# Rotating the latent queries of a two-layer encoder: the exchange of halves as copies out of PSUM instead of a product, with the rotated dimensions projected first

## The chip, the cores and the metric

The kernel runs on one core of one Trainium2 chip. The core's engines work side by side, each through its own queue of instructions in a fixed order: TensorE (PE, matrix products into the 8 banks of PSUM), VectorE (DVE), ScalarE (ACT), GpSimd (POOL) and SyncE (SP), which here issues nearly all of the transfers. The metric is the device time of one execution in microseconds (us), as a median over runs.

## The reference

The model is a bidirectional encoder trunk of two layers on 256 tokens of width 2048, all in fp32. In each layer four heads of differential attention and eight heads of latent attention share an input projection and an output projection; a dense MLP with squared ReLU follows, and every sublayer is modulated by a conditioning vector `c`. The part that the change touches is the latent attention's query: 512 latent columns `cq` are normalised and projected to eight heads of 128 plain ("nope") and 64 rotated dimensions.

```python
q = (_rmsnorm(cq, q_norm_g[l]) @ w_uq[l]).reshape(B, S, MLA_HEADS, MLA_NOPE + MLA_ROPE)
q_nope = q[..., :MLA_NOPE]
q_rope = _rope(q[..., MLA_NOPE:], cos[:, :, None, :], sin[:, :, None, :])
...
def _rope(x, cos, sin):
    half = x.shape[-1] // 2
    x1, x2 = x[..., :half], x[..., half:]
    out = jnp.concatenate([x1 * cos - x2 * sin, x2 * cos + x1 * sin], axis=-1)
    return out.astype(x.dtype)
```

So each 64-vector is split into halves of 32, which change places for the sine's term. The scores are `(q_nope . k_nope + q_rope . k_rope) / sqrt(192)`, with one rotated key `k_rope` for all heads. `mod = silu(c) @ w_ada[l] + b_ada[l]` gives the modulation, 12288 values in each layer.

## The kernel before

**Weights.** fp32 precision is had from three products of a faster format: each 1 MB weight tile `raw` comes by one transfer (issued by SyncE) and is split in two halves of 128x1024. ScalarE writes the rounded `hi` (L148), VectorE the remainder `lo = raw - hi` (L151), and PE multiplies `hi` with the rounded activation, `hi` with its remainder and `lo` with the rounded activation (L187 to L189; L258 to L260 where the tokens are the stationary side). `weights()` does the load and the split. There are 5 `raw` buffers and 4 each of `hi` and `lo`.

**The modulation runs beside the rest.** `w_ada` is 192 tiles of 1 MB, called `ada`, which use the same 5 buffers as `raw`. VectorE multiplies each with `silu(c)` and sums it (L304), and after every second tile adds the bias to `mod` (L315, L317). Each call of `weights()` does two things at its end: `ada_sums(ins)` sums all `ada` tiles loaded so far and orders those sums behind the second `lo` of this weight; then `self.credit += self.rate` decides how many new `ada` loads are issued behind it. The rate is set by stage: 0.7 in most of layer 0, 2.7 while `up_q(0)` loads its weight there, 1.7 in the value stages. So where a weight stands in the program also decides where `ada` loads stand in SyncE's queue and where their sums stand in VectorE's.

**The place of the change.** In each layer, after the differential heads' scores, the program goes through these steps: `up_k()` projects the plain keys; `probs(3)` is the softmax of the last differential head; `up_q(0)` projects the plain query dimensions of the first four latent heads; `turn(0)` transposes the first head's probabilities (PE into bank `pt`, L1187, then a copy `aT`); `up_r()` projects all rotated query dimensions, 4 x 128 columns in two banks `pss`, copies each bank to `qr` on ScalarE with the scale of the scores (`copy`, L277), and calls `rope_q` on it; `turn(1)`; `mla[0]()`, the first latent head's scores; `up_v()`, the latent value weights `w_uv` (banks `pv`, copies `vm`); the next heads; `up_q(1)`; and then the differential values, eight weights `w_dv` interleaved with the other latent heads, called the value stage below.

`rope_q` (L1131 to L1141) exchanges the halves by a product on PE with a constant 128x128 permutation, kept among the constants that one transfer brings (tile `tab`): the fp32 product takes `qr` 128x512 into a bank `pqr` (L1135). VectorE multiplies that bank with the sine into `qrt` (L1138), `qr` with the cosine (L1139), and adds the two (L1140).

`mla_steps` writes a latent head's scores into one bank `psm` in two halves of 128 queries: plain part (L1235, `kn`, `qn`), rotated part (L1236, `kr`, `qr`), and VectorE negates and reduces each half into `sm` (L1237). ScalarE's exponential follows (L1149). The second half's product and the first half's reduction use the same bank, and PE waits for that reduction before it goes on with the second half.

**The order.** Each engine's order is fixed when the program is built. In layer 0 a scheduler with its own estimates of durations interleaves the steps, within the dependencies; `follow(ins, after)` adds one by hand, without a semaphore, for order alone. In layer 0 the `hi` copies of `w_uv` follow `self.copied`, the last call of `copy`.

Of the kernel before, what the change touches and what calls it, by code (L numbers as in the profile page):

```python
# [13 lines left out]
AF = mybir.ActivationFunctionType  # L14
ALU = mybir.AluOpType
AX = mybir.AxisListType

P = 128
# [21 lines left out]
]  # L40

C_DELTA = 0
C_PERM = 32
C_CB = 160
C_W2 = 168
C_FREQ = 176
C_SGN = 177
NCONST = 178

V_BADA = 0  # L50
V_SUBLN = 192
# [19 lines left out]
def consts():  # L71
    c = np.zeros((P, NCONST), np.float32)
    p = np.arange(P)
    c[p, C_DELTA + p % 32] = 1.0
    c[p, C_PERM + (p ^ 32)] = 1.0
    for g in range(8):
        for r in range(4):
            b = 4 * g + r
            n = b % 16
            lo, hi = BUCKET_FROM[n], BUCKET_FROM[n + 1] - 1  # L80
            sign = -1.0 if b < 16 else 1.0
            rows = slice(32 * r, 32 * r + 32)
            if b == 16:
                c[rows, C_CB + g], c[rows, C_W2 + g] = 0.0, 0.0
            else:
                c[rows, C_CB + g] = -sign * (lo + hi) / 2.0
                c[rows, C_W2 + g] = 1.0 if n < 8 else ((hi - lo) / 2.0 + 0.25) ** 2
    c[:, C_FREQ] = np.asarray(INV_FREQ, np.float32)[p % 32]
    c[:, C_SGN] = np.where(p % 64 < 32, -1.0, 1.0)
    return c  # L90
# [13 lines left out]
class Trunk:  # L104
# [231 lines left out]
    def setup(self):  # L336
# [4 lines left out]
        nc.sync.dma_start(row, io["c"])  # L341
        tab = cp.tile([P, T + 8 + NCONST + NVEC], F32, name="tab")
        nc.scalar.dma_start(tab, io["tab"])
        self.pos = tab[:, : T + 8].bitcast(I32)
        self.K = tab[:, T + 8 : T + 8 + NCONST]
        self.vec = tab[:, T + 8 + NCONST :]
        self.x = cp.tile([P, NK, T], F32, name="x")
# [94 lines left out]
    def bias_part(self, a):  # L442
# [8 lines left out]
        for g in order[:4]:  # L451
            sqs.append(self.t("sq"))
            ins = nc.scalar.activation(sqs[-1], r, AF.Square, bias=K[:, C_CB + g : C_CB + g + 1])
        if a < 3:
            self.rel[a + 1] = self.distances(a + 1)
        self.bias_out(ins)
        for g in order:
            if g % 4 > 1:
                sq = sqs.pop(0)
            else:  # L460
                sq = self.t("sq")
                nc.scalar.activation(sq, r, AF.Square, bias=K[:, C_CB + g : C_CB + g + 1])
            oh = half("oh", F32R)
            flat, edge = sq.rearrange("p a b -> p (a b)"), K[:, C_W2 + g : C_W2 + g + 1]
            if g % 4 < 2:
# [27 lines left out]
    def rope_setup(self):  # L493
# [3 lines left out]
        nc.vector.tensor_copy(ang, pos[:, :T])  # L497
        nc.vector.tensor_scalar(ang, ang, K[:, C_FREQ : C_FREQ + 1], None, ALU.mult)
        magic = 1.5 * 2.0**23
# [15 lines left out]
        nc.scalar.activation(self.cos, c, AF.Sin)  # L515
        nc.vector.tensor_scalar(self.sin, self.sin, K[:, C_SGN : C_SGN + 1], None, ALU.mult)

# [187 lines left out]
    def layer(self, l, acc, st):  # L705
        nc, io = self.nc, self.io
        qs = 1.0 / math.sqrt(128.0)
        ms = 1.0 / math.sqrt(192.0)
# [16 lines left out]
        else:  # L725
            h = acc
            lat = []
            for b in range(0, NAHEAD, 2):
                t, c = self.scaled(st, b, self.u("cr"))
# [6 lines left out]
        cq, ckv = [], []  # L736
        kk, qn, kn, qr, vm, a, at, v, o = [], [], [], [], [], [], [], [], []
# [16 lines left out]
        def up_k():  # L754
            kn.extend(self.copy(ps, "kn") for ps in self.small(io["w_uk"][l], ckv, 8))
# [2 lines left out]
            qn.extend(self.copy(ps, "qn", ms) for ps in self.small(io["w_uq"][l, b], cq, 4))  # L758

        def up_r():  # L760
            raw = [self.copy(ps, "qr", ms) for ps in self.small(io["w_uq"][l, 2], cq, 4)]
            qr.extend(self.rope_q(x) for x in raw)

        def up_v():
            w = self.weights(io["w_uv"][l], after=None if l else self.copied)
            for cg in range(2):
                pss = [self.bank("pv") for _ in range(2)]
                self.tokens_by_k(pss, [[z[:, 512 * cg : 512 * cg + 512] for z in y] for y in w], ckv, True, True)
                vm.append([self.copy(ps, "vm") for ps in pss])
# [12 lines left out]
        def probs(hd):  # L782
            return lambda: a.append(self.diff_probs(l, self.diff_scores(hd, q[hd], kk[hd])))

        def turn(hd):
            return lambda: at.append(self.transposed(a[hd]))
# [47 lines left out]
            self.rate = RATE_A2  # L834
        up_k()
        probs(3)()
        rate = self.rate
        if l == 0:
            self.rate = RATE_Q
        up_q(0)  # L840
        self.rate = rate
        turn(0)()
        up_r()
        turn(1)()
        mla[0]()
        if l == 0:
            self.rate = RATE_A3
        up_v()
        turn(2)()
        for f in mla[1:3]:  # L850
# [277 lines left out]
            nc.vector.tensor_tensor(out[s, i], t[s, 0], t[s, 1], ALU.add)  # L1128
        return out

    def rope_q(self, raw):  # L1131
        nc = self.nc
        ps = self.bank("pqr")
        flat = lambda x: x.rearrange("p a b -> p (a b)")
        nc.tensor.matmul(flat(ps), self.K[:, C_PERM : C_PERM + P], flat(raw), start=True, stop=True)  # L1135
        t = self.t("qrt")
        wide = lambda x: x.unsqueeze(1).broadcast_to([P, 2, T])
        nc.vector.tensor_tensor(t, ps, wide(self.sin), ALU.mult)  # L1138
        nc.vector.tensor_tensor(raw, raw, wide(self.cos), ALU.mult)  # L1139
        nc.vector.tensor_tensor(raw, raw, t, ALU.add)  # L1140
        return raw  # L1141
# [144 lines left out]
def _layout(i):  # L1286
# [13 lines left out]
    vec += [np.stack([f[f"diff_lambda_{a}{j}"][l] for a in "qk" for l in range(2) for j in (1, 2)], 1)]  # L1300
    vec += [np.repeat(f["rel_bias_table"].reshape(8, 4, HD).transpose(1, 0, 2).reshape(4, 32), 32, 0)]
    a["tab"] = np.concatenate([pos.view(np.float32), consts()] + vec, 1)
    assert a["tab"].shape == (P, T + 8 + NCONST + NVEC)
    a["fg"] = np.ascontiguousarray(np.broadcast_to(f["final_norm_g"], (P, D)))
# [51 lines left out]
```

## Time and profile before

| | |
|---|---|
| median of 3 runs | 2191.54 us (2191.27 to 2192.47) |
| the profiled execution | 2190.2 us, of it 2188.4 us span |
| PE busy | 2158.3 us, 99% of the span |
| VectorE busy | 1610.4 us, 74% |
| ScalarE busy | 1153.3 us, 53% |
| bytes moved | 586.41 MB, mean 268 GB/s |

Times inside the program are counted from the span's start. A row of a timeline has the start, the duration, the engine, the line, the operation, and its output and inputs by name; a bracket gives the idle time of that engine just before it and what ended it. The fp32 products are recorded in several parts, so that four records belong to two products. The chain of waits is followed back from the last instruction; its pieces don't overlap, where records of pipelined products do. PEclk is the share of its full clock that TensorE was granted. The rotation stands at 219.7 us (layer 0) and 1282.9 us (layer 1).

### The profile page before, as it was taken

To read this page: it belongs to the slowest core of one execution; us is meant where nothing else is said; L and a number is where in the kernel's file an instruction comes from. 1 tells how busy PE (TensorE), PEld (TensorE's weight loads), DVE (VectorE), ACT (ScalarE), POOL (GpSimd) and SP (SyncE) were. 2 spreads that over 40 slices of the span, in tenths; PEclk is the share of its full clock that TensorE was granted. 3 is DMA by queue.
4 is the path that set the end of the run, shared out by engine and by line. 5 is a ranking of instruction groups with operands and counts; after the bars stand their busy time and mean duration, and the time that the engine had idled before them with its cause. 6 is when DMAs were issued, how large, how long until landed. Compare 5 with 4: busy or idle time off the path is not lost.

```text
span 2188.4 us, 30328 instructions
## 1 busy us (share of the span) xinstructions
PE 2158.3 (99%) x11984; PEld 1889.1 (86%) x11984; DVE 1610.4 (74%) x2162; ACT 1153.3 (53%) x1737; POOL 23.8 (1%) x43
## 2 busy tenths in 40 slices
PE   8999999999999999999999999999999999999998
PEld 6899889998888888888898888999888888888886
DVE  8988978888678788788798876798545545545566
ACT  6555664454455355355456565647446535534544
POOL 0000000000000000000001000000000000000000
PEclk9999999999999999999999999999999999999999
DMA  9986888799888889888867666687555555555552
GB/s 399 414 309 249 345 327 293 265 359 353 310 319 325 329 302 341 322 312 319 312 231 271 251 249 231 233 306 247 190 195 185 191 195 188 188 193 192 189 196 95
DMA packets 85538, 586.41 MB, mean 268 GB/s; under 512 B 9489, under 2 KB 9489, under 8 KB 19345
## 3 DMA queue, kind: packets, MB, share of 16 engines
q1 hardware_dynamic: 85106, 583.84, 72.6%
q8 instruction: 94, 1.54, 0.3%
q10 hardware_dynamic: 288, 0.62, 0.1%
q14 instruction: 50, 0.41, 0.1%
HBM read 582.32 MB, written 2.10 MB: 267 GB/s over the span
## 4 chain that ended last, share of the span: by engine, by line
PE 91%; DVE 5%; ACT 2%; issue 0%; DMA 0%; DVEq 0%; ACTq 0%
PE ps L208 24%; PE ps L211 13%; PE py L1061 11%; PE py L1059 11%; PE py L1063 11%; DVE ada L304 3%; PE pk L189 2%; PE pk L187 2%; PE pk L188 2%; PE pv L258 2%; PE pv L259 2%; PE pv L260 2%; PE pa L189 1%; PE pa L187 1%; PE pa L188 1%; DVE lo L151 1%
## 5 line engine op out<-in xcount | busy, mean ns | idle before, releaser
L151 DVE TENSOR_TENSOR lo<-raw,hi 128x1024 fp32r<-128x1024 f32 (+1 forms) x720 | 849.4, 1194 | 473.9 <-ACT hi L148 302.5
L148 ACT ACTIVATE hi<-raw 128x1024 fp32r<-128x1024 f32 (+1 forms) x720 | 737.6, 1035 | 646.4 <-PE py L1063 357.3
L208 PE MATMUL ps<-h,hi 128*128 128x512 f32 x2016 | 471.0, 390 | 0.9 <-ACT hi L148 0.9
L208 PEld LDWEIGHTS ps<-h,hi 128*128 128x128 f32 x2016 | 375.0, 188 | 76.9 <-ACT hi L148 1.3
L304 DVE SCALAR_TENSOR_TENSOR ada<-ada,cond 128x2048 f32<-128x2048 f32 x192 | 437.5, 2284 | 3.1 <-DMA ada<-in_w_ada 3.1
L1059 PE MATMUL py<-hi,hid 128*128 128x512 f32 x1024 | 326.5, 390 | 0.0
L1061 PE MATMUL py<-lo,hid 128*128 128x512 f32 x1024 | 325.9, 389 | 0.0
L1063 PE MATMUL py<-hi,hid 128*128 128x512 f32 x1024 | 325.7, 389 | 0.0
L211 PEld LDWEIGHTS ps<-h,lo 128*128 128x128 f32 x2016 | 250.2, 192 | 4.9
L211 PE MATMUL ps<-h,lo 128*128 128x256 f32 x2016 | 251.7, 283 | 0.0
L1061 PEld LDWEIGHTS py<-lo,hid 128*128 128x128 f32 x1024 | 192.3, 188 | 40.3 <-DVE lo L151 0.4
L1063 PEld LDWEIGHTS py<-hi,hid 128*128 128x128 f32 x1024 | 192.2, 188 | 40.0
L1059 PEld LDWEIGHTS py<-hi,hid 128*128 128x128 f32 x1024 | 191.3, 188 | 38.8
L1098 ACT ACTIVATE sum<-ps 128x256 f32<-128x256 f32 x110 | 42.0, 382 | 122.4 <-PE ps L211 122.4
L187 PE MATMUL pk<-h,hi 128*128 128x256 f32 x304 | 87.4, 293 | 5.2 <-ACT hi L148 3.6
L189 PE MATMUL pk<-h,lo 128*128 128x256 f32 x304 | 87.3, 291 | 1.2 <-DVE lo L151 1.1
L188 PE MATMUL pk<-h,hi 128*128 128x256 f32 x304 | 87.3, 289 | 0.0
L181 DVE TENSOR_TENSOR hid<-relu,hid 128x256 fp32r<-128x256 f32 x128 | 48.3, 421 | 45.8 <-ACT hid L180 45.8
L244 PE MATMUL pk<-hf,w 128*128 128x256 f32 x288 | 64.8, 386 | 6.1 <-ACT hf L654 6.1
L244 PEld LDWEIGHTS pk<-hf,w 128*128 128x128 f32 x288 | 55.5, 194 | 14.7 <-ACT hf L654 6.9
L187 PEld LDWEIGHTS pk<-h,hi 128*128 128x128 f32 x304 | 59.8, 199 | 6.2 <-ACT hi L148 4.4
L189 PEld LDWEIGHTS pk<-h,lo 128*128 128x128 f32 x304 | 59.6, 197 | 2.1 <-DVE lo L151 2.0
(267 smaller groups left out, 2553.3 us busy)
## 6 DMA issues: line engine op xcount, KB each, us to landing
raw<-in_w_m SPq DMA_DIRECT2D x238, 1024.0 KB, 5.0
ada<-in_w_ada SPq DMA_DIRECT2D x192, 1024.0 KB, 5.1
raw<-in_w_ob SPq DMA_DIRECT2D x24, 1024.0 KB, 5.0
raw<-in_w_dv SPq DMA_DIRECT2D x16, 1024.0 KB, 4.8
raw<-in_w_q SPq DMA_DIRECT2D x16, 1024.0 KB, 4.8
raw<-in_w_n SPq DMA_DIRECT2D x16, 768.0 KB, 6.1
w<-in_w_a SPq DMA_DIRECT2D x24, 384.0 KB, 12.6
raw<-in_w_a SPq DMA_DIRECT2D x12, 768.0 KB, 6.2
```

What stands on the lines that cost most here:

```text
L148: ins = nc.scalar.activation(hi, v, AF.Copy)
L151: ins = nc.vector.tensor_tensor(lo, v, hi.bitcast(F32), ALU.subtract)
L187: mm(ps, hi, x[0], start=first, stop=False, skip_group_check=shared)
L188: mm(ps, hi, x[1], start=False, stop=False, skip_group_check=shared)
L189: mm(ps, lo, x[0], start=False, stop=last, skip_group_check=shared)
L208: mm(ps.rearrange("p a b -> p (a b)"), part(w, 0, k), both, start=k == 0, stop=False)
L211: mm(ps[:, 0], part(w, 1, k), x, start=False, stop=k == nk - 1)
L244: self.nc.tensor.matmul(ps, w[i][:, j * P : j * P + P], whole[i], start=first, stop=last, skip_group_check=True)
L304: ins = nc.vector.scalar_tensor_tensor(w, w, 1.0, self.cond, ALU.mult, ALU.mult, accum_out=acc[:, i : i + 1])
L1059: mm(o, xh[:, tok], hi[:, part[j]], start=start, stop=False)
L1061: mm(o, xh[:, tok], lo[:, part[j]], start=False, stop=False)
L1063: mm(o, xl[:, tok], hi[:, part[j]], start=False, stop=stop)
```

## The change

There are three edits.

1. `rope_q` takes the PSUM bank itself. It copies it to `qr` as before, and then copies each group of 32 partitions, with the scale, into the neighbouring group of a new SBUF tile `qrt`: four copies of 32x512 on ScalarE in place of the product. VectorE's product with the sine now reads and writes `qrt`. The permutation leaves the constants, which shrink from 690 to 562 columns.
2. `up_r()`, and with it `turn(0)`, now stand ahead of `up_q(0)` in both layers. Layer 0's rate of 2.7 still belongs to `up_q(0)`'s weight alone.
3. In layer 0 the `hi` copies of the latent value weights follow `self.spun`, the last exchange copy, instead of `self.copied`.

```diff
-C_PERM = 32
...
-    c[p, C_PERM + (p ^ 32)] = 1.0
...
         def up_r():
-            raw = [self.copy(ps, "qr", ms) for ps in self.small(io["w_uq"][l, 2], cq, 4)]
-            qr.extend(self.rope_q(x) for x in raw)
+            qr.extend(self.rope_q(ps, ms) for ps in self.small(io["w_uq"][l, 2], cq, 4))
 
         def up_v():
-            w = self.weights(io["w_uv"][l], after=None if l else self.copied)
+            w = self.weights(io["w_uv"][l], after=None if l else self.spun)
...
         up_k()
         probs(3)()
+        up_r()
+        turn(0)()
         rate = self.rate
         if l == 0:
             self.rate = RATE_Q
         up_q(0)
         self.rate = rate
-        turn(0)()
-        up_r()
         turn(1)()
         mla[0]()
...
-    def rope_q(self, raw):
-        nc = self.nc
-        ps = self.bank("pqr")
-        flat = lambda x: x.rearrange("p a b -> p (a b)")
-        nc.tensor.matmul(flat(ps), self.K[:, C_PERM : C_PERM + P], flat(raw), start=True, stop=True)
-        t = self.t("qrt")
+    def rope_q(self, ps, scale):
+        nc = self.nc
+        raw, t = self.copy(ps, "qr", scale), self.t("qrt")
+        for i in range(4):
+            to, at = slice(32 * (i ^ 1), 32 * (i ^ 1) + 32), slice(32 * i, 32 * i + 32)
+            self.spun = nc.scalar.activation(t[to], ps[at], AF.Copy, scale=scale)
         wide = lambda x: x.unsqueeze(1).broadcast_to([P, 2, T])
-        nc.vector.tensor_tensor(t, ps, wide(self.sin), ALU.mult)
+        nc.vector.tensor_tensor(t, t, wide(self.sin), ALU.mult)
         nc.vector.tensor_tensor(raw, raw, wide(self.cos), ALU.mult)
         nc.vector.tensor_tensor(raw, raw, t, ALU.add)
         return raw
```

The order that each engine gets from this follows for two places in layer 0. In these rows a number behind a name tells one tile from the next of its kind, and "x2" is two rows of one form; lines after the change are numbered two or three lower.

VectorE, around the rotation. Before, from the end of the plain projection's `lo` on, where `ada_388` to `ada_390` are three modulation tiles, `lo_419` and `lo_421` the value weights, `psm_412` the first latent head's scores:

```order
L304 SCALAR_TENSOR_TENSOR ada_388_2012,macc02_84<-ada_388_2012,cond_103 128x2048
L304 SCALAR_TENSOR_TENSOR ada_389_2014,macc02_84<-ada_389_2014,cond_103 128x2048
L304 SCALAR_TENSOR_TENSOR ada_390_2016,macc02_84<-ada_390_2016,cond_103 128x2048
L317 TENSOR_TENSOR mod02_83<-macc02_84,tab_106 128x2
L1138 TENSOR_TENSOR qrt_407_2149<-pqr_406_2147,sin_1228 128x512
L1139 TENSOR_TENSOR qr_403_2118<-qr_403_2118,cos_1227 128x512
L1138 TENSOR_TENSOR qrt_409_2155<-pqr_408_2153,sin_1228 128x512
L1140 TENSOR_TENSOR qr_403_2118<-qr_403_2118,qrt_407_2149 128x512
L1139 TENSOR_TENSOR qr_405_2145<-qr_405_2145,cos_1227 128x512
L151 TENSOR_TENSOR lo_419_2185<-raw_417_2182,hi_418_2184 128x1024
L1140 TENSOR_TENSOR qr_405_2145<-qr_405_2145,qrt_409_2155 128x512
L1237 TENSOR_SCALAR sm_413_2167,mxm_414_2168<-psm_412_2166 128x256
```

After, from the second rotation's operations on, where the same three tiles are `ada_401` to `ada_403`, the value weights `lo_417` and `lo_419`, and `psm_410` and `psm_432` the first and second latent head's scores:

```order
L1135 TENSOR_TENSOR qrt_393_2074<-qrt_393_2074,sin_1228 128x512
L1137 TENSOR_TENSOR qr_392_2072<-qr_392_2072,qrt_393_2074 128x512
L149 TENSOR_TENSOR lo_417_2185<-raw_415_2182,hi_416_2184 128x1024
L1234 TENSOR_SCALAR sm_411_2167,mxm_412_2168<-psm_410_2166 128x256
L149 TENSOR_TENSOR lo_419_2189<-raw_415_2182,hi_418_2188 128x1024
L1234 TENSOR_SCALAR sm_411_2167,mxm_412_2168<-psm_410_2166 128x256
L302 SCALAR_TENSOR_TENSOR ada_401_2099,macc02_84<-ada_401_2099,cond_103 128x2048
L1151 RECIPROCAL r_414_2176<-tot_413_2175 128x2
L302 SCALAR_TENSOR_TENSOR ada_402_2101,macc02_84<-ada_402_2101,cond_103 128x2048
L302 SCALAR_TENSOR_TENSOR ada_403_2103,macc02_84<-ada_403_2103,cond_103 128x2048
L315 TENSOR_TENSOR mod02_83<-macc02_84,tab_106 128x2
L1234 TENSOR_SCALAR sm_433_2244,mxm_434_2245<-psm_432_2243 128x256 x2
```

The three sums moved from ahead of the rotation to behind the value weights' two `lo` and the first head's reductions, and the reductions of `psm_432` stand behind them.

On ScalarE the copies of the rotated dimensions with the exchange now come ahead of those of the plain ones, and the value weights' first `hi` stands between the two plain copies, the second behind the transposed probabilities.

SyncE's loads (`in_w_uq` are the query weights, `in_w_uv` the value weights). Before:

```order
L163 DMA raw_383_2000<-in_w_uq 128x2048
L294 DMA ada_388_2012<-in_w_ada 128x2048
L294 DMA ada_389_2014<-in_w_ada 128x2048
L294 DMA ada_390_2016<-in_w_ada 128x2048
L163 DMA raw_397_2079<-in_w_uq 128x2048
L163 DMA raw_417_2182<-in_w_uv 128x2048
L294 DMA ada_422_2192<-in_w_ada 128x2048
L294 DMA ada_423_2194<-in_w_ada 128x2048
L163 DMA raw_441_2262<-in_w_uq 128x2048
```

After:

```order
L161 DMA raw_383_2000<-in_w_uq 128x2048
L161 DMA raw_396_2089<-in_w_uq 128x2048
L292 DMA ada_401_2099<-in_w_ada 128x2048
L292 DMA ada_402_2101<-in_w_ada 128x2048
L292 DMA ada_403_2103<-in_w_ada 128x2048
L161 DMA raw_415_2182<-in_w_uv 128x2048
L292 DMA ada_420_2196<-in_w_ada 128x2048
L292 DMA ada_421_2198<-in_w_ada 128x2048
L161 DMA raw_439_2266<-in_w_uq 128x2048
```

The second query weight moved ahead of the three `ada` loads; the loads behind them keep their order.

More of the change, by code (lines that the diff above doesn't have):

```diff
@@ L42 @@
 C_DELTA = 0
-C_PERM = 32
[L44 to L48, printed above, removed]
+C_CB = 32
+C_W2 = 40
+C_FREQ = 48
+C_SGN = 49
+NCONST = 50
 V_BADA = 0
```

## The prediction

> **What bounds the kernel now.** I read the page first: the busy times, and the chain that ended last.
>
> ```profile
> span 2188.4 us, 30328 instructions
> PE 2158.3 (99%) x11984; PEld 1889.1 (86%) x11984; DVE 1610.4 (74%) x2162; ACT 1153.3 (53%) x1737; POOL 23.8 (1%) x43
> PE 91%; DVE 5%; ACT 2%; issue 0%; DMA 0%; DVEq 0%; ACTq 0%
> ```
>
> TensorE is busy 99% of the span and is 91% of the chain. A microsecond of products removed is a microsecond of time, unless TensorE then waits for what was hidden behind those products. The changed place recurs in both layers, so I read the chain there and what PE waits for.
>
> ```profile
> 219.85 1.81 PE pqr L1135 x4
> ```
> ```profile
> 1283.02 1.97 PE pqr L1135 x4
> ```
> ```profile
> PE pv L258 <- ACT hi L148: 1.2, 1, 1.2
> ...
> PE psm L1235 <- DVE sm L1237: 0.5, 1, 0.5
> ```
>
> Both pairs of rotation products (four records each) lie on the chain: 1.81 us in layer 0, 1.97 in layer 1. Each is followed by one wait: 1.20 us for the first half of the value weights (layer 0), 0.53 for a score half that VectorE reduces (layer 1; the full list has no other such wait). Those four numbers, 5.51 us, are all that this place can give.
>
> Next, the stretches of layer 0 from the products to the end of the value stage, since most of what moves lies there.
>
> ```profile
> core 0: us, PE busy (x) PEld busy (x) DVE busy (x) ACT busy (x) POOL busy (x), PEclk, DMA share, GB/s
> 220.00:240.00 20.00, 18.80 (x111) 15.79 (x110) 16.98 (x30) 14.55 (x28) 0.00 (x0) 1.00 0.90 346
> 240.00:260.00 20.00, 20.00 (x97) 16.76 (x96) 18.49 (x30) 11.46 (x25) 0.00 (x0) 1.00 0.83 320
> 260.00:280.00 20.00, 20.00 (x93) 16.69 (x92) 17.26 (x32) 13.29 (x27) 0.00 (x0) 1.00 0.93 362
> 280.00:300.00 20.00, 20.00 (x96) 16.77 (x95) 17.27 (x23) 8.58 (x16) 0.00 (x0) 1.00 0.83 305
> ```
>
> PE is gapless from 240 to 300, but VectorE is busy 86 to 92% and the DMA engines 83 to 93%. This stretch is covered with little to spare, so later weights may show.
>
> **The change part by part.** *The product goes.* The tile's rows:
>
> ```profile
> L1135 PE MATMUL pqr<-qr,tab x8: 590/592/697, 219.7 to 1284.4; 128*128 128x512 f32 x8
> L1138 DVE TENSOR_TENSOR qrt<-pqr,sin x4: 683/684/684, 221.4 to 1285.7; 128x512 f32<-128x512 f32 x4
> L1139 DVE TENSOR_TENSOR qr<-qr,cos x4: 682/683/685, 222.0 to 1286.9; 128x512 f32<-128x512 f32 x4
> L481 ACT ACTIVATE bias<-pb x16: 570/588/593, 42.5 to 85.9; 32x512 f32<-32x512 f32 x16
> ```
>
> Eight PE records leave. By the chain that is -1.81 and -1.97 us, -3.78 together (records overlap, so the chain's pieces count, not 8 x 0.592).
>
> *The exchange.* Sixteen ScalarE copies of 32x512 from PSUM arrive, eight in each layer. Their like stands in the trace: L481 copies 32x512 from a bank's group of 32 partitions to another group of 32, at 588 ns. Four are 4 x 0.59 = 2.35 us, with the 0.60 of `qr` about 3 us for each half of the projection.
>
> ```profile
> 217.01 0.60 ACT L277 ACTIVATE qr<-pss 128x512 f32<-128x512 f32 x1 [2.28 <-PE pss L189]
> 219.89 0.60 ACT L277 ACTIVATE qr<-pss 128x512 f32<-128x512 f32 x1 [2.28 <-PE pss L189]
> 222.14 0.60 ACT L277 ACTIVATE aT<-pt 128x512 f32<-128x512 f32 x1 [1.65 <-PE pt L1187]
> 222.63 2.00 ACT L148 ACTIVATE hi<-raw 128x1024 fp32r<-128x1024 f32 x2
> ```
>
> A half of the projection takes 2.88 us on PE (217.01 to 219.89), and ACT sat idle for 2.28 us of each. So the copies end about when the next half does, and the rest falls beside the nope projection, which now comes after. I cost them at nothing on the path. Cover gone, it would be one half's excess, about 0.1 us, and above that 3 us at most if the rotation came last again.
>
> *The first factor from SBUF.* VectorE's product with the sine read PSUM (684 ns); now it reads SBUF, as the cosine's does (683). So six rotation operations cost what they cost, 6 x 0.60 us by their starts. [...]
>
> *The constants* lose 128 of 690 columns. The table's load is 345 KB, landing in 2.9 us by the row below, so at most 2.9 x 128/690 = 0.5 us of a first stretch in which other transfers run too; bounds 0 and -0.5, I take -0.1.
>
> ```profile
> tab<-in_tab ACTq DMA_DIRECT2D x1, 345.0 KB, 2.9
> ```
>
> *The order in layer 0.* What VectorE did before:
>
> ```profile
> 213.52 1.22 DVE L151 TENSOR_TENSOR lo<-raw,hi 128x1024 fp32r<-128x1024 f32 x1
> 214.65 2.28 DVE L304 SCALAR_TENSOR_TENSOR ada<-ada,cond 128x2048 f32<-128x2048 f32 x1
> ...
> 221.29 0.16 DVE L317 TENSOR_TENSOR mod<-macc,tab 128x2 f32<-128x2 f32 x1
> 221.36 0.68 DVE L1138 TENSOR_TENSOR qrt<-pqr,sin 128x512 f32<-128x512 f32 x1
> ...
> 226.10 0.42 DVE L1237 TENSOR_SCALAR_CACHE_REDUCE sm<-psm 128x256 f32<-128x256 f32 x1
> ```
>
> Three `ada` sums (214.65 to 221.29, 2.21 us each) ran under the projections, at a time when the rotation was not ready. After the change the rotation stands ahead of them, then the two `lo` of the value weights and two score reductions, and only then the three sums, with the first reduction of the next score pair (`psm_432`) behind them. PE can't do that pair's second half until this reduction has read the bank.
>
> The other durations of the walk, from the chain (PE) and ScalarE's timeline:
>
> ```profile
> 221.66 0.45 PE pt L1187 x4
> ...
> 227.16 0.43 PE psm L1235 x2
> ...
> 228.02 0.23 PE pv L258
> ```
> ```profile
> 226.11 1.06 ACT L148 ACTIVATE hi<-raw 128x1024 fp32r<-128x1024 f32 x1 [1.49 <-DMA raw<-in_w_uq]
> 227.08 0.49 ACT L1149 ACTIVATE sm<-sm,mxm 128x256 f32<-128x256 f32 x1
> ```
>
> The first nope half's copy takes the place of `qr`'s at 217.0, so the first `hi` of the value weights ends near 217.5 + 1.06 = 218.6. The second half of the nope projection ends at 219.85, where the product began. `aT` and the second `hi` (1.06) of the value weights end near 221.9, its `lo` (1.22) at 223.1, one reduction at 223.5, the sums at 223.5 + 3 x 2.21 = 230.1, `mod` 230.2, the reduction 230.7. PE from 219.85: transpose 0.44, two score halves of 0.86, 24 value products of 0.23 (5.52), transpose 0.44, the first half 0.86, transpose 0.44: 229.3. It waits 1.4 us. The next `hi` of `up_q(1)` then stands on ScalarE behind an exponential (0.5) that needs the same reduction: 230.7 + 0.5 + 1.06 = 232.2, against PE at 230.7 + 0.86 = 231.55, so 0.65 more. I put 0.25 on its second half, between 0 and the 0.7 that PE lacks if that `hi` follows another exponential. New waits: 2.3. Before's 1.20 goes, since the first value half is now ready (218.6) before PE asks for it. So up to here -1.81 - 1.20 + 2.30 = **-0.7 us**.
>
> *What the sums free.* Each `ada` tile is one of five 1 MB buffers that the weights use too, and SyncE issues their loads in program order.
>
> ```profile
> 219.18 0.33 SPq L163 DMA_DIRECT2D raw<-in_w_uq  x1
> ...
> 280.70 0.33 SPq L163 DMA_DIRECT2D raw<-in_w_dv  x1
> ```
> ```profile
> 285.45 2.01 ACT L148 ACTIVATE hi<-raw 128x1024 fp32r<-128x1024 f32 x2 [3.35 <-DMA raw<-in_w_dv]
> ```
> ```profile
> 289.63 0.58 PE L258 MATMUL pv<-hi,h 128*128 128x512 f32 x1
> ```
>
> The weights of `up_q(1)` were issued at 219.18; their buffer is now freed by the first late sum, 225.75, 6.6 later. Behind that stand all loads of the value stage. VectorE lacked work for 8 to 14% of this stretch, and so catches part of it up: walking on in the same way I get the seventh value load about 4.6 us late (285.3 for 280.70). Before, ScalarE took that tile the moment it landed (after 3.35 us of waiting), was done with its first half near 286.5, and PE wanted it at 289.63: 3.1 us of cushion, 2.4 for a PE that comes 0.7 earlier. The exposed wait is 4.6 - 2.4 = 2.2; the bounds are 0 (VectorE uses its idle time) and 2.2. I take 1.4, nearer the walked figure than nothing. Layer 0: -0.7 + 1.4 = **+0.7 us**, from -3.0 to +1.5.
>
> *Layer 1* keeps its order of `lo` and sums. It gains the product, -1.97. The score half may stand behind one `lo` (1.22) where PE comes sooner: 0 to 1.22, I take 0.5, which before's own 0.53 suggests; of that 0.53, half goes. So -1.97 + 0.5 - 0.27 = **-1.75**, from -2.5 to -0.8.
>
> *Sum:* +0.7 - 1.75 - 0.1 = -1.15 us on the profiled execution (2190.2, of it 2188.4 span). The median of the runs shown is 2191.54, 1.3 above that execution; I put the difference on the median: **2190.4**.
>
> **The rivals.** 0.2% is 4.4 us, about what a measurement of this kernel can tell from no change.
>
> *All cover holds (0.18).* The scheduler of layer 0 had these durations too roughly, and VectorE's idle time takes the lag: no new waits. Then -1.81 - 1.20 - 1.97 - 0.53 - 0.1 = -5.6 us, 2185.9. For it: ScalarE is 53% busy. Against it: the sums now stand between a bank and its reader, and 6.6 us of VectorE don't vanish.
>
> *Late loads (0.15), slower.* SyncE takes one thing at a time: should one more pair of `ada` loads stand ahead of the seventh value load, waiting for its two sums (4.4 us), the lag is 9.0 instead of 4.6 and the exposed wait 6.6. Layer 0 is then +5.9, all +4.1 us: 2195.6. It decides from where the exposed wait passes 0.7 + 1.75 + 0.1 = 2.55 us, that is with the seventh load issued after 280.70 + 2.4 + 2.55 = 285.7. For it: a DMA share up to 0.93, and ScalarE waits for value loads in this stretch already (230 to 330 us):
>
> ```profile
> ACT hi L148 <- DMA raw<-in_w_dv: 4.4, 3, 3.3
> ```
>
> Against it: PE had no wait there.
>
> *The clock falls (0.05).* Where PE idles in several short pieces, the trace shows this (408 to 416 us, from its wait of 1.53, the longest of three there, on):
>
> ```profile
> 408.39 1.65 PE L187 MATMUL pk<-h,hi 128*128 128x256 f32 x6 [1.53 <-ACT h L649]
> ```
> ```profile
> 408.00:410.00 2.00, 1.61 (x7) 1.62 (x8) 2.00 (x6) 1.18 (x3) 0.00 (x0) 0.50 0.44 184
> ...
> 414.00:416.00 2.00, 2.00 (x17) 2.00 (x17) 2.00 (x4) 0.75 (x2) 0.00 (x0) 0.87 0.00 0
> ```
>
> About 6 us at half clock and 2 at 0.87: 3.0 + 0.3 = 3.3 us lost. My waits of 1.4, 0.65 and 0.25 resemble those, but full products stand between them. With the fall: -1.15 + 3.3 = +2.1, 2193.7. In 220 to 240 the clock held 1.00 through the 1.20 wait. [...]
>
> That the product doesn't go can't be: the order of PE has no such row left.
>
> **How the numbers follow.** Forecast 0.62, the rivals 0.18, 0.15 and 0.05. Faster by over 0.2% needs four fifths of the full gain: two thirds of the first rival and little else, 0.13. Slower by over 0.2% is the upper half of late loads: 0.07. Within: 0.80. The range goes from near the first rival's value to near the second's, 2186.2 to 2195.0, leaving about 0.1 on each side.
>
> **What would show it.** Right: no `pqr` in either layer; 16 copies at about 0.59 us; PE near 229 waiting 1.4 us for the reduction behind three sums, then 0.65 for `hi`; a PE wait near 289 of 1 to 2 us; layer 1 gaining 1 to 2.5 us between the products' place and the end of `up_q(1)`. Wrong: VectorE doing the sums earlier than the order's place (it can't), the seventh value load issued near 281 (then all cover holds) or after 285.7 (late loads), PEclk under 1.00 in 225 to 240, or a time changed outside these two places by over 1 us.

## The result and the profile after

The changed kernel takes 2196.09 us (median of 12 runs, 2194.74 to 2197.96), the kernel before 2191.40 in the same comparison (12 runs, 2188.64 to 2192.47): ratio 1.0025, 95% interval 1.0017 to 1.0032. That is 4.7 us slower, where 1 us faster was forecast, and 1.1 us beyond the range's upper end.

The page's first lines show the odd thing about it: PE's busy time is what it was (2158.9 for 2158.3 us), and the span is longer by 6.8. The medians lie only 4.7 apart: these are two single executions, and the clock, in the last section, is part of their difference.

```profile
span 2195.2 us, 30331 instructions
PE 2158.9 (98%) x11976; PEld 1889.6 (86%) x11976; DVE 1612.1 (73%) x2162; ACT 1161.6 (53%) x1753; POOL 20.4 (1%) x43
PE 88%; DVE 6%; ACT 3%; DMA 1%; issue 1%; DVEq 0%; ACTq 0%
```

To see where, I cut both traces at instructions that both kernels have: A, the first product of `up_k()` in layer 0 (into `pss`); B, the first product of the output projection's second part there (into `ps`); C, the first `pss` product in layer 1; and the span's end. All the starts are read off PE's timeline.

| stretch, us | before | after | difference |
|---|---|---|---|
| start to A | 200.20 | 202.64 | +2.44 |
| A to B: layer 0 from the latent keys to the output projection | 136.19 | 142.74 | **+6.55** |
| B to C: rest of layer 0, MLP, start of layer 1 | 926.78 | 925.68 | -1.10 |
| C to the end: layer 1's place and what follows | 925.23 | 924.14 | **-1.09** |

The change does next to nothing up to A (a shorter table of constants); the 2.44 there is the clock's, and the last section returns to it. The -1.10 from B to C is the clock's too, and so no sign against the prediction, which had named a change of over 1 us outside its two places as one: behind the same wait of 1.53 us at the MLP's norm the mean PEclk was 0.76 before (404 to 418 us) and 0.88 after (413 to 427), and to PE's next wait it took 68.90 us before and 67.89 after. Layer 0 lost 6.55 us in the place of the change, layer 1 gained 1.09. Between A and B PE waits five times, where before it waited once, for 1.20 us. Its timeline has the waits in brackets:

```profile
233.07 0.70 PE L1232 MATMUL psm<-kn,qn 128*128 128x256 f32 x2 [1.34 <-DVE sm L1234]
234.65 0.38 PE L185 MATMUL pss<-lath,hi 128*128 128x256 f32 x1 [0.45 <-ACT hi L146]
...
270.59 0.73 PE L256 MATMUL pv<-hi,h 128*128 128x512 f32 x2 [0.35 <-ACT hi L146]
...
295.14 0.33 PE L1184 MATMUL pt<-ident,sm 128*128 128x128 f32 x1 [1.74 <-ACT sm L1237]
...
314.01 0.39 PE L185 MATMUL pk<-mo,hi 128*128 128x256 f32 x1 [2.85 <-ACT hi L146]
```

The first two are those walked out in the prediction (1.4 and 0.65). VectorE's timeline shows the order at work: the first and the last of three sums, and behind them the reduction that PE waits for; the same again with two sums 63 us later, where PE gets its transposition only through that reduction, an exponential and a scaling.

```profile
225.82 2.29 DVE L302 SCALAR_TENSOR_TENSOR ada<-ada,cond 128x2048 f32<-128x2048 f32 x1
...
230.31 2.29 DVE L302 SCALAR_TENSOR_TENSOR ada<-ada,cond 128x2048 f32<-128x2048 f32 x1
...
232.59 0.42 DVE L1234 TENSOR_SCALAR_CACHE_REDUCE sm<-psm 128x256 f32<-128x256 f32 x1
...
288.40 2.29 DVE L302 SCALAR_TENSOR_TENSOR ada<-ada,cond 128x2048 f32<-128x2048 f32 x1
...
290.61 2.29 DVE L302 SCALAR_TENSOR_TENSOR ada<-ada,cond 128x2048 f32<-128x2048 f32 x1
...
292.89 0.42 DVE L1234 TENSOR_SCALAR_CACHE_REDUCE sm<-psm 128x256 f32<-128x256 f32 x1
```

Before, the reduction near there stood ahead of the sums:

```profile
291.12 0.42 DVE L1237 TENSOR_SCALAR_CACHE_REDUCE sm<-psm 128x256 f32<-128x256 f32 x1
...
291.47 2.29 DVE L304 SCALAR_TENSOR_TENSOR ada<-ada,cond 128x2048 f32<-128x2048 f32 x1
```

SyncE's issues of the weights of `up_q(1)` and of the seventh value weights, on a clock that is 2.44 late at A:

```profile
228.15 0.33 SPq L161 DMA_DIRECT2D raw<-in_w_uq  x1
...
288.51 0.33 SPq L161 DMA_DIRECT2D raw<-in_w_dv  x1
```

They were 219.18 and 280.70. Less the 2.44, the first is 6.5 us late (forecast 6.6) and the second 5.4 (forecast 4.6), past the 5.0 (285.7) that the rival "late loads" named as its point.

The longest wait has two causes in sight, a late weight and ScalarE's order at the end of the value stage. That order, after and before:

```profile
309.23 1.28 ACT L275 ACTIVATE v<-pv 128x512 f32<-128x512 f32 x2 [7.70 <-PE pv L258]
...
311.16 1.28 ACT L1202 ACT_TABLE_LOAD   x1
...
312.92 1.04 ACT L146 ACTIVATE hi<-raw 128x1024 fp32r<-128x1024 f32 x1
```
```profile
302.47 1.28 ACT L277 ACTIVATE v<-pv 128x512 f32<-128x512 f32 x2 [5.07 <-PE pv L260]
303.64 1.05 ACT L148 ACTIVATE hi<-raw 128x1024 fp32r<-128x1024 f32 x1
```

In the kernel before, the first output weight's `hi` stood right behind the two `v` copies; now a table load of 1.28 us and five other operations stand between. The weight itself was issued at 303.28 and took 8.3 us to land (before: 296.47 and 5.5), so it was there at 311.6, after the `v` copies but 1.3 us before its `hi` began. And behind that wait the clock fell:

```profile
core 0: us, PE busy (x) PEld busy (x) DVE busy (x) ACT busy (x) POOL busy (x), PEclk, DMA share, GB/s
...
314.00:316.00 2.00, 1.95 (x8) 1.55 (x9) 1.22 (x1) 2.00 (x6) 0.00 (x0) 0.80 0.10 41
316.00:318.00 2.00, 2.00 (x8) 1.73 (x7) 1.23 (x1) 1.14 (x5) 0.00 (x0) 0.50 0.00 0
318.00:320.00 2.00, 2.00 (x16) 2.00 (x16) 1.99 (x2) 1.79 (x4) 0.00 (x0) 0.85 0.90 254
```

By these rows 1.95 x 0.20 + 2 x 0.50 + 2 x 0.15 = 1.7 us of PE's work at most. A run below (order only) has the same wait of 2.85 us without the fall (PEclk 1.00 in 316 to 322): from its end to B it took 30.21 us, the changed kernel 31.37, so the fall cost nearer 1.2.

### The profile page after: what moved, and what is told of

It reads as the page before. It is cut to its first block, busy times and chain, and to the rows that moved or that the text cites. A ratio compares the mean times of both kernels' runs of the same rounds, so it can differ in the third digit from the quotient of the medians.

```text
span 2195.2 us, 30331 instructions
## 1 busy us (share of the span) xinstructions
PE 2158.9 (98%) x11976; PEld 1889.6 (86%) x11976; DVE 1612.1 (73%) x2162; ACT 1161.6 (53%) x1753; POOL 20.4 (1%) x43
## 4 chain that ended last, share of the span: by engine, by line
PE 88%; DVE 6%; ACT 3%; DMA 1%; issue 1%; DVEq 0%; ACTq 0%
PE ps L206 24%; PE ps L209 13%; PE py L1058 11%; PE py L1056 11%; PE py L1060 11%; DVE ada L302 3%; PE pv L256 1%; PE pk L187 1%; PE pv L258 1%; PE pk L185 1%; PE pv L257 1%; PE pk L186 1%; PE pk L242 1%; DVE lo L149 1%; PE pa L187 1%; PE pa L185 1%
```

## The experiments

Theory "late sums": the new order puts three modulation sums behind the value weights, in front of a reduction that PE needs, and holds up the loads behind them. Rival "busy ScalarE": the added copies make the weights' `hi` late. All ratios are against the kernel before in the same comparison, with 95% intervals; the differences named below are between those two medians. A to B is the stretch of the table above, from one traced execution each, and a fall of the clock is in it: in "changed kernel", "order only" and "copies, no burst" of 1.7 us at most, an estimate from their PEclk as the one above, in "copies only" and "first follow" of about twice that.

| run | median, us | before, us | ratio | A to B, us |
|---|---|---|---|---|
| kernel before | | | 1 | 136.19 |
| changed kernel | 2196.09 | 2191.40 | 1.0025 (1.0017 to 1.0032) | 142.74 |
| copies only | 2191.47 | 2190.63 | 1.0006 (0.9997 to 1.0015) | 139.96 |
| order only | 2199.41 | 2190.63 | 1.0043 (1.0030 to 1.0056) | 145.51 |
| rate with the place | 2193.17 | 2190.63 | 1.0012 (1.0003 to 1.0021) | 139.00 |
| layer 1 only | 2189.00 | 2190.63 | 0.9989 (0.9980 to 0.9999) | 136.19 |
| first follow | 2197.96 | 2190.16 | 1.0033 (1.0021 to 1.0046) | 145.84 |
| no burst | 2190.80 | 2190.16 | 1.0006 (0.9997 to 1.0015) | 134.34 |
| copies, no burst | 2196.06 | 2190.16 | 1.0029 (1.0019 to 1.0040) | 141.97 |
| fewer loads | 2199.02 | 2190.16 | 1.0040 (1.0027 to 1.0054) | 133.60 |
| loads spread | 2183.55 | 2191.22 | 0.9969 (0.9958 to 0.9980) | 133.50 |
| spread, one less | 2186.30 | 2191.22 | 0.9982 (0.9973 to 0.9991) | 134.33 |
| before, spread | 2189.14 | 2191.22 | 0.9997 (0.9988 to 1.0006) | 138.02 |
| spread, values too | 2195.80 | 2191.22 | 1.0023 (1.0012 to 1.0034) | 134.66 |

**Copies only** (the exchange, in the old order).

```diff
-        up_r()
-        turn(0)()
         rate = self.rate
...
         up_q(0)
         self.rate = rate
+        turn(0)()
+        up_r()
         turn(1)()
...
-after=None if l else self.spun
+after=None if l else self.copied
```

> The exchange by copies alone: up_r() stays behind up_q(0), the value weights' hi copies follow the last copy as before, and the three modulation sums stay ahead of the rotation. Theory 'late sums' (the loss comes from the three sums that moved behind the value weights, and from the loads that their buffers hold up): no new wait of PE, both products gone (-1.8 and -2.0 us), perhaps the 1.2 us wait for the value weights left: 3.5 to 5.5 us faster than before. Rival 'busy ScalarE' (sixteen added copies make the hi of the weights late and so everything behind them): about as slow as the changed kernel in layer 0, net between 0 and 4 us slower than before.

Measured: 0.8 us slower, not told apart from before. The number lies in the range of "busy ScalarE"; that of "late sums" (3.5 to 5.5 us faster) failed. PE's one wait in A to B, and VectorE's rows in front of it:

```profile
225.56 1.19 PE L1233 MATMUL psm<-kr,qr 128*128 128x256 f32 x2 [3.78 <-DVE qr L1137]
```
```profile
220.14 2.28 DVE L302 SCALAR_TENSOR_TENSOR ada<-ada,cond 128x2048 f32<-128x2048 f32 x1
...
222.43 0.68 DVE L1135 TENSOR_TENSOR qrt<-qrt,sin 128x512 f32<-128x512 f32 x1
...
224.12 0.69 DVE L1135 TENSOR_TENSOR qrt<-qrt,sin 128x512 f32<-128x512 f32 x1 [0.41 <-ACT qrt L1133]
224.73 0.68 DVE L1137 TENSOR_TENSOR qr<-qr,qrt 128x512 f32<-128x512 f32 x1
```

The rotation stands behind the three sums as it did before, and VectorE ends its first half nearly when it did (this trace is 1.07 us late at A; 225.41 less that is 224.3, before it was 223.8). PE only arrives earlier: the product's 1.81 us and the 1.20 us wait turned into one wait of 3.78 for VectorE. In the kernel before, the product on PE was cover for VectorE's sums. The copies have a smaller share in the wait: behind the sums VectorE waits 0.41 us for the second half's, and the addition that PE needs stands behind that. And the wait cost more than itself: PEclk was 0.65, 0.50, 0.50 and 0.65 in 224 to 232. In 226 to 230:

```profile
226.00:228.00 2.00, 2.00 (x6) 1.53 (x6) 2.00 (x4) 1.19 (x2) 0.00 (x0) 0.50 1.02 430
228.00:230.00 2.00, 2.00 (x9) 1.60 (x8) 1.23 (x3) 1.91 (x4) 0.00 (x0) 0.50 0.13 53
```

**Order only** (the product stays).

```diff
+        up_r()
+        turn(0)()
         rate = self.rate
...
         up_q(0)
         self.rate = rate
-        turn(0)()
-        up_r()
         turn(1)()
```

> The order alone: the product with the permutation stays, up_r() and the first transposition stand ahead of up_q(0). VectorE's and SyncE's order are then nearly those of the changed kernel. Theory 'late sums': the same waits in layer 0 as in the changed kernel, with the products' 3.8 us on top: 6 to 9 us slower than before. Rival 'busy ScalarE': no added copies, so no change within 1.5 us.

Measured: 8.8 us slower; the waits are those of the changed kernel (1.76 and 0.45, 1.74, 2.85 us), with one of 0.53 in front of them and one of 0.20 behind, and without that of 0.35. The order alone brings the loss, and a busy ScalarE can't be it, since no copy was added. This run also parts the two causes of the longest wait:

```profile
raw<-in_w_oa SPq DMA_DIRECT2D x1, 1024.0 KB, 6.9
```
```profile
314.79 1.04 ACT L148 ACTIVATE hi<-raw 128x1024 fp32r<-128x1024 f32 x1
```
```profile
315.89 0.39 PE L187 MATMUL pk<-mo,hi 128*128 128x256 f32 x1 [2.85 <-ACT hi L148]
```

The output weight, issued at 305.14, was there at 312.0, and its `hi`, behind the same table load, began 2.8 us later. So here the whole wait is ScalarE's order and not the load. All loads of the value stage are later than in the changed kernel (the seventh 9.3 us behind before's, for 5.4), and the waits are the same.

**Rate with the place** (the rate of 2.7 at `up_r()`).

```diff
-        up_r()
-        turn(0)()
         rate = self.rate
         if l == 0:
             self.rate = RATE_Q
-        up_q(0)
+        up_r()
         self.rate = rate
+        turn(0)()
+        up_q(0)
         turn(1)()
```

> The change whole, but the rate of 2.7 moves with the place, from up_q(0) to up_r(): the three modulation loads are again issued behind the first of the two query weights and summed behind the lo of the second, ahead of the value weights. Theory 'late sums': SyncE's order is that of before, the waits for the reduction (1.3 us), the late value loads and the waits near 295 and 314 us go: 4 to 6 us faster than before. Rival 'busy ScalarE': as slow as the changed kernel, 3 to 5 us slower than before.

Measured: 2.5 us slower, 2 us better than the changed kernel in size, between the two expectations. The value loads were hardly earlier than in the changed kernel, against the theory (the seventh value load is issued at 286.83, on a clock 1.25 late at A, so 4.9 us behind before's). Yet the waits of 1.74 and 2.85 were gone, with 0.69, 0.66, 0.53 and 0.18 in their place. The sums now stand between the rotation's operations and ahead of the first head's reduction, and PE waited longest for that:

```profile
226.89 0.70 PE L1232 MATMUL psm<-kn,qn 128*128 128x256 f32 x2 [2.04 <-DVE sm L1234]
```

Three sums are 6.6 us of VectorE; without the product's cover something was late behind them in each of the three places tried here (copies only, the changed kernel, this run).

**Layer 1 only.** Layer 0 keeps product and order: `if l:` around the new order and the new rotation.

> The change in layer 1 alone (order and copies); layer 0 keeps product and order. Both theories: layer 1 gains 1.5 to 2.5 us by the traces (2.2 us between the two profiles), so 1.5 to 2.5 us faster than before. If the loss lay in layer 1, the kernel would be slower.

Measured: 1.6 us faster, at the low end; by its trace C to the end is 0.9 us shorter. Layer 1 gains, and less than its product.

**First follow** (the third edit undone).

```diff
-after=None if l else self.spun
+after=None if l else self.copied
```

> The change whole, but layer 0's value weights' hi copies follow the last call of copy again and not the last exchange copy. The three sums and the loads stand as in the changed kernel. Theory 'late sums': within 1.5 us of the changed kernel, 3 to 6 us slower than before. Rival 'the third edit' (the hi that now stands between the two plain copies does the harm): back at before or faster, -3 to 0 us.

Measured: 7.8 us slower, worse than the changed kernel. The third edit does no harm: without it a wait of 0.53 us and one of 1.80 (for 1.34) came at the score halves, one of 0.72 in the value stage, and the clock fell behind the 1.80 too (PEclk 0.50 in 234 to 236).

**No burst** (one modulation load at `up_q(0)` in place of three).

```diff
-RATE_Q = 2.7
+RATE_Q = 0.7
```

> The change whole, but the rate at up_q(0) is 0.7 instead of 2.7, so that one modulation load stands there instead of three and one sum stands ahead of the second head's reduction; the two missing loads are caught up at the end of layer 0's attention, where a few tenths to 2 us of wait may come. Theory 'late sums': the waits of 1.3 and 0.45 us at 233 to 235 go, value loads about 4 us earlier than in the changed kernel, the waits near 295 and 314 shrink: 5 to 8 us faster than the changed kernel, 1 to 4 us faster than before. If the sums' place is innocent: as the changed kernel, 4 to 5 us slower than before.

Measured: 0.6 us slower than before, so about 4 us better than the changed kernel, each against its own comparison's before; both totals of the theory (1 to 4 us faster than before, 5 to 8 than the changed kernel) failed. In A to B the theory held: 134.34 us, 8.4 less than the changed kernel and 1.85 less than before, with waits of 0.53 and 0.22 in all. What it won there it paid at the MLP's norm, where the two missing loads were caught up; PE's timeline has 3.7 us of waits there, of which this is the first:

```profile
461.65 0.98 PE L185 MATMUL pk<-h,hi 128*128 128x256 f32 x6 [1.22 <-ACT h L647]
```

**Copies, no burst** (the same rate in the copies only).

> The exchange by copies in the order of before, again with a rate of 0.7 at up_q(0). In the run of the copies alone PE waited 3.8 us for the rotation behind the three sums, and its clock fell. Theory 'the products covered the sums' (the rotation stands behind sums that PE used to wait out under the products): with one sum less than 2 us of wait are left and no fall of the clock, 3 to 5 us faster than the copies alone, 2 to 4 us faster than before. If the copies on ScalarE made the rotation late: the wait of about 3.8 us stays, as the copies alone.

Measured: 5.9 us slower, A to B 141.97: the expectation failed. The wait for the rotation did shrink, from 3.78 to 0.90 us, as "the products covered the sums" says. What is left of it is the copies' doing: the first sum comes only at 226.71, and VectorE waits for ScalarE:

```profile
219.04 0.69 DVE L1135 TENSOR_TENSOR qrt<-qrt,sin 128x512 f32<-128x512 f32 x1 [1.72 <-ACT qrt L1133]
```

But waits of 0.53 for a reduction and 1.22 for a weight's `hi` followed close behind, the clock fell again (0.55 and 0.60 in 224 to 228), and further waits of 2.2 us came in the value stage and behind it. In the old order the exchange by copies came too late for PE with three sums ahead of it and with none.

**Fewer loads** (the changed kernel, rate 1.2 in the value stage).

```diff
-RATE_A3 = 1.7
+RATE_A3 = 1.2
```

> The change whole, but the rate in the value stage is 1.2 instead of 1.7: the three sums stand where they do in the changed kernel, fewer modulation loads stand between the value loads, and they are caught up at the end of layer 0's attention. Theory 'late loads': the waits of 1.3 and 0.45 us at 233 to 235 stay, those near 270, 295 and 314 us (0.35, 1.74, 2.85) and the fall of the clock behind the last go: 4 to 6 us faster than the changed kernel, within 1.5 us of before. Rival (those waits come from the order of ScalarE and VectorE, not from loads): they stay in part, less than 2 us faster than the changed kernel.

Measured: in A to B 133.60 us, 9.1 less than the changed kernel, and one wait of 0.38 us at 230. The waits at 270, 295 and 314 are gone, and by the length of the stretch the fall of the clock: before's 136.19 less the product's 1.81 and the wait of 1.20, with 0.38 added, is 133.56 already. The 1.34 went too, since the scheduler gave PE other work there. As a whole it was 8.9 us slower than before, where within 1.5 us was expected: five loads were missing, and at the norm PE waited 1.5, 3.4 and 3.3 us for modulation, besides smaller ones.

**Loads spread** (the count ahead of the value weights kept, one load at each weight instead of three at once).

```diff
-RATE_A0, RATE_Q = 0.7, 2.7
+RATE_A0, RATE_Q = 1.0, 0.7
```

> The change whole, with the modulation loads spread: rate 1.0 instead of 0.7 in the input projection of layer 0, where VectorE and the DMA engines have room, and 0.7 instead of 2.7 at up_q(0). One load stands at each weight there, the count up to the value weights is kept, and nothing has to be caught up at the end of the attention. Theory 'late sums and loads': no wait at 233 to 235, the waits near 270, 295 and 314 gone as in the run without the burst (0.75 us were left there), and none of its 3.7 us at the MLP's norm: 3 to 5.5 us faster than before, 8 to 10 faster than the changed kernel. If the gain without the burst came only from loads left out: 0 to 5 us slower than before.

Measured: 7.7 us faster than before (6.8 by the ratio, 0.9969 with 0.9958 to 0.9980), more than the 3 to 5.5 expected. All of PE's list of waits that concerns scores and transpositions, in both layers, is now this:

```profile
PE psm L1232 <- DVE sm L1234: 0.8, 2, 0.5
PE psm L1232 <- ACT qn L275: 0.8, 1, 0.8
```

A to B is 133.50, 9.2 less than in the changed kernel and 2.7 less than before. The loads are not put off: by B VectorE has summed 62 tiles, before it was 61. B to C is 924.39, 2.4 less than before; the waits of 0.65 and 0.92 us that PE had there for two weights' `hi` (477 and 487 us) are gone.

**Spread, one less** (rate 0.9 in place of 1.0).

> As the spread loads, with rate 0.9: one load fewer ahead of the value weights, and one to catch up later. Expected within 1.5 us of the spread loads; where their place and not their number decides, either may be ahead.

Measured: 4.9 us faster than before, 2.8 behind the spread loads. That is more than the 1.5 expected for one load.

**Before, spread** (the kernel before with rates 1.0 and 0.7).

> The kernel before with the same rates as the spread loads (1.0 and 0.7): product and old order kept. It tells how much of the spread kernel's time is the rates' and how much the change's. Theory: the burst stood well covered under the products in the kernel before, so the rates alone bring little, between 1 us faster and 1.5 us slower than before. Rival (the burst cost something in every order): 2 us or more faster than before.

Measured: 0.9997 (0.9988 to 1.0006), 0.7 us faster by the ratio and 2.1 by the medians. The interval (2.6 us faster to 1.3 slower) reaches into the theory's range and the rival's, so how much the rates alone give is not settled. They don't act in one place: A to B is 1.8 us longer than before, with waits of 2.15 us, and B to C 3.5 shorter (923.28). At equal rates the change is worth 2189.14 - 2183.55 = 5.6 us by the medians. In the traces that is 138.02 - 133.50 = 4.5 us in A to B and 1.1 from C on (925.25 to 924.14), while B to C is 1.1 longer and the start 1.7 shorter (198.77 us for 200.45), where the clock fell in one of the two: from the end of the wait near 129 us to A it is 69.5 us in the spread loads and 70.4 or more in this run.

**Spread, values too** (rates 1.0, 1.0 and 1.5).

> The change whole with rate 1.0 in the input projection, 1.0 at up_q(0) and 1.5 instead of 1.7 in the value stage: about two loads moved from the value stage to ahead of it. Theory 'late loads': the value loads come earlier still and PE has no wait there; 3 to 6 us faster than before, if the output projection takes the rest in; if loads must be caught up at the norm, 1 to 3 us less.

Measured: 4.6 us slower than before; the expectation failed. A to B was much as foreseen (134.66, with waits of 0.53 and 0.61 us), but PE waited 1.2 us at 404, 1.2 at 438 and 2.7 at 477 us, and the stretch B to C rose to 935.19.

## Why the prediction was wrong

**Right in kind.** The product's 1.81 us left the chain in layer 0 (from A to the transposition behind the projections, 1.87 us less), the 1.20 us wait went, and the two waits behind the three sums came at 1.34 and 0.45 us for 1.4 and 0.65. The copies cost 589 ns each, and VectorE's products with the sine 693 ns from SBUF for 684 from PSUM:

```profile
L1133 ACT ACTIVATE qrt<-pss x16: 586/589/596, 214.6 to 1290.4; 32x512 f32<-32x512 f32 x16
```

**Where it failed: the step "What the sums free".** It gave the lag of the value loads one place to show, the seventh load at 289 us, and so a wait between 0 and 2.2 us, of which it took 1.4. The lag was about right (5.4 us for 4.6), but no wait came there. Measured were 0.35 + 1.74 + 2.85 = 4.94 us at three other places, and a fall of the clock behind the last. What the step left out is that the engines' orders changed far behind the place of the change too. On VectorE two later sums stand ahead of a later reduction (288.40 to 292.89). On ScalarE the first output weight's `hi` stands behind a table load. My walk ended before 290 and never looked at the end of the value stage. The two long waits come with these orders, whatever the lateness of the loads: they are the same with the seventh value load 5.4 us late (changed kernel) and 9.3 late (order only), and gone with it 4.9 late under other orders (rate with the place). Of the 2.85 in the changed kernel the late weight alone would have cost an estimated 1.5 (PE idle from 311.16, the weight there at 311.6, 1.04 for its `hi`); in order only, where it was there 2.8 us early, next to nothing. The wait of 0.35 is a late value weight, for whose transfer ScalarE waited (0.30 us, up to 269.48). The runs without the burst, with fewer loads and with spread loads show that the orders hang on how many modulation tiles stand there; why the scheduler wrote these, the runs don't show.

The sum for layer 0 by the trace, with the fall of the clock at 1.2: -1.87 - 1.20 + 1.34 + 0.45 + 4.94 + 1.2 = +4.9 of the +6.55. The rest, 1.7 us, I couldn't assign.

**Layer 1: the step that costed the exchange at nothing on the path.** Forecast -1.75, measured -0.5 to -1.2 in the kernels with the copies (-1.09 in the changed one). The step read layer 0's rows of before, where ScalarE takes each half of the rotated projection as it ends and is idle between, and took that for both layers. In the changed kernel's layer 1 PE has ended both halves when it transposes at 1284.56, and only then does ScalarE begin, behind a weight's `hi`:

```profile
1284.56 0.60 PE L1184 MATMUL pt<-ident,a 128*128 128x128 f32 x4
```
```profile
1283.97 1.06 ACT L146 ACTIVATE hi<-raw 128x1024 fp32r<-128x1024 f32 x1 [1.99 <-issue]
1284.93 0.57 ACT L275 ACTIVATE qr<-pss 128x512 f32<-128x512 f32 x1
1285.54 2.39 ACT L1133 ACTIVATE qrt<-pss 32x512 f32<-32x512 f32 x4
1287.95 0.60 ACT L275 ACTIVATE qr<-pss 128x512 f32<-128x512 f32 x1
1288.57 2.39 ACT L1133 ACTIVATE qrt<-pss 32x512 f32<-32x512 f32 x4
1290.98 0.60 ACT L275 ACTIVATE aT<-pt 128x512 f32<-128x512 f32 x1
1291.48 0.59 ACT L275 ACTIVATE qn<-pss 128x512 f32<-128x512 f32 x1
```

Eight exchange copies and two `qr` copies then run back to back to 1290.96, about as long as PE's whole plain projection beside them (1284.91 to 1290.76), and these copies are on the chain. PE then waits 0.77 us for that `qn` and 0.26 for a reduction, where 0.53 was before: -1.97 + 0.77 + 0.26 - 0.53 = -1.5; the 0.4 that is missing to -1.09 isn't assigned. The 3 us of copies for each half were right; that they fall beside PE's own halves was not.

**The rivals.** "Late loads" had the right sign, the sign it named came true (issue after 285.7; it was 286.1 on before's clock), and its time, 2195.6, is nearly the measured one. That the time fits is luck: it was to come from a lag of 9.0 us and one wait of 6.6 for the seventh value weight, where the lag was 5.4 and the long waits came from the orders. "The clock falls" I had put at 225 to 240, where the clock held 1.00; it fell at 314. It was wrong to take the rivals as alternatives, since a wait and a fall of the clock behind it came together here (2.85 us, then PEclk 0.50 in 316 to 318). "All cover holds" was refuted here. With the loads spread the change gave its 5.6 us, but not by its sum: layer 1 gave 1.1 of them for the 2.5 in that sum.

## What to carry to other kernels

A product that PE spends in front of another engine's late work may be that work's cover: before you remove it, ask what the next product needs and when the engine behind it is done, for here the exchange alone brought a wait of 3.78 us in place of 1.81 of products and 1.20 of wait. A step that moves carries along whatever is tied to its place, here three 1 MB loads and 6.6 us of VectorE; settle first where those belong. Walk a lag on to the end of the stretch that shares its buffers, read every engine's order there and not at the changed place alone, and price a wait of PE with and without a slow clock behind it (here the fall behind 2.85 us cost an estimated 1.2 more).

## What the runs showed of the hardware

The clock's fall is not settled by the length of one wait. It fell behind recorded waits of 3.78 us (copies only, down to 0.50), of 1.80 and of 1.76 with 0.45 behind them (first follow and order only, mean PEclk 0.72 in 232 to 238 and in 234 to 240), and of 0.90, 0.53 and 1.22 close together (copies, no burst; 0.55 in 224 to 226). It did not fall behind one of 2.04 (rate with the place, PEclk 1.00 in 224 to 234) or of 1.34 with 0.45 (changed kernel, 1.00 in 230 to 240). And the same wait goes both ways: behind 2.85 us the clock fell in the changed kernel (the rows at 314 above) and in first follow (0.72 in 314 to 320), and not in order only, where the wait ends at 315.89:

```profile
316.00:322.00 6.00, 5.97 (x44) 5.56 (x45) 5.18 (x6) 5.65 (x13) 0.00 (x0) 1.00 0.33 93
```

How long the clock stays low differs from trace to trace behind the same wait. All fourteen kernels have one of 2.4 us that ends near 129 to 131 us. The 12 us from 128 on in spread loads, before and after:

```profile
128.00:140.00 12.00, 10.12 (x82) 9.91 (x83) 11.66 (x24) 7.53 (x10) 0.00 (x0) 1.00 0.90 338
```
```profile
128.00:140.00 12.00, 10.49 (x73) 10.29 (x74) 11.34 (x22) 6.05 (x8) 0.00 (x0) 0.86 0.81 320
```
```profile
128.00:140.00 12.00, 9.27 (x52) 9.07 (x53) 10.66 (x21) 5.48 (x8) 0.00 (x0) 0.72 0.90 355
```

From the end of this wait to A it is 69.5 and 69.8 us in the two traces without a fall (spread loads; copies, no burst), 70.4 to 71.6 in the nine like before, and 72.0 to 72.5 in the three like after. So one wait cost nothing, about 1.3 or about 2.6 us of clock. By this the traces of before and after are 1.2 us apart at A. The other 1.2 of the 2.44 is there when the wait ends (128.95 and 130.17), behind a stretch from 25 to 35 us where the mean PEclk was 0.81 before and 0.66 after. The twelve runs of the kernel before lie between 2188.64 and 2192.47; that such falls make part of this spread is likely, and not shown. For differences of a few microseconds the stretches between common instructions tell more than two spans, and a fall of the clock has to be looked for in them too.
